# A two-layer diffusion backbone on one core: row steps of the modulation placed behind the weight splits of the convolution, and some weight splits given to VectorE

## The chip, the cores and the metric

One core of a Trainium2 chip runs the whole kernel. The metric is the device time of one execution in microseconds. Beside it there is one execution taken by the hardware profiler, whose trace gives the start, the duration and the idle time ahead of each instruction.

## The reference

A block of two layers over 1024 latent tokens and 256 context tokens, each 1024 wide, in float32. Both streams are scaled and shifted by a modulation computed from a conditioning vector. Cut to what matters here:

```python
for layer in range(2):
    mod = silu(c) @ mod_w[layer] + mod_b[layer]            # six rows of 1024: shifts, scales, gates
    h = modulate(rms_norm(xs, norm1_g[layer]), sh1, sc1)   # hc for the context, with modc
    if layer == 0:   # gate_b, gate_c, u, q_lat, kv_lat, k_rope = split(h @ w_in)
        y = concat(gate_b * conv3(gate_c * u), latent_attention(q_lat, kv_lat, k_rope)) @ w_out
    else:
        y = window_attention(h @ w_qkv) @ w_out
    xs = xs + g1 * y
    h2 = modulate(rms_norm(xs, norm2_g[layer]), sh2, sc2)
    aff = softmax(h2 @ router_w[layer])                    # 16 experts, each takes its best 128 tokens
    g, idx = top_k(aff.T, 128)
    hid = silu(h2[idx] @ w_gate) * (h2[idx] @ w_up)        # 1024 -> 1024 for each expert
    xs = xs + g2 * scatter_add(idx, (hid @ w_down) * g)
return rms_norm(xs, final_g)                               # in layer 0 the context goes the same way
```

## The kernel before

Every float32 operand of a product is split in two: a high half (`wh`, `hh`, `xh`), which ScalarE makes by a cast, and a low half (`wl`, `hl`, `xl`), which is the operand less the high half, a subtraction on VectorE (`dve.tensor_sub`) or on GpSimd (`pool.tensor_sub`). A product is then three matmuls (`mm3`, L167 to L170): low weight by high activation, high by high, high by low. `hilo` (L163 to L165) is the pair of instructions for one tile.

The stages follow each other: the mixer of layer 0 (convolution, then latent attention), `mixer_out` of layer 0 with the routing, 16 experts, then the same in layer 1 with window attention. In the mixer of layer 0, in both `mixer_out` and in the last stage (`finish`, L2415) all queues run in the order in which the program is written. In the experts of layer 0 only TensorE and GpSimd do, and a planner lays out the other engines by its costs; in the experts of layer 1 the planner lays out everything up to `finish`. Behind the loop over the experts (L1904 and on) it lays out layer 0's queues as well.

*Start and convolution (`layer0_conv`, L415 to L655).* The tokens stand in five groups of 256 columns (`Group`); `Group.parts` (L473) scales a transposed group out of PSUM: ScalarE writes the high half (L480), VectorE writes the full value h (L484), VectorE or GpSimd subtracts (L486). The input weights come in four chunks of 384 columns and one of 416 (`Chunk`); `Chunk.parts` (L500) splits two of the eight k-blocks of a chunk, a piece. The pieces of the first chunk are split ahead of the loop, by GpSimd (L542 to L558), between the modulation's columns and the parts of the first group, and the norm of the second group (`between`, taken up a step at a time by `aside`) is started among them. The loop (L575) goes over four chunks j and over five groups g: `proj(1, g)` and `proj(2, g)` give z (L632), `proj(0, g)` gives the gate (L604), and `taps` the three-point convolution (L598 to L600). The next chunk's first two pieces are split at g = 3 (L641), the last two behind the last projection, ahead of gate(4) (L647).

Beside it the loop works off a list, `rest` (L571): eight units of TensorE for one modulation part, and four rows of modulation on VectorE. A row has four steps of four instructions (L353, `use`), each with one load in a ring of six slots, and at the end a sum over partitions by TensorE with an addition by VectorE (L361, L363, `sum`). `proj` counts its calls, and at about every second one it takes the next unit of `rest` (L590 to L593), right behind its own matmuls are queued. What is left is worked off behind the loop (L654).

*Queries (L808 to L816).* The value weights wv are split by `hilo`; the key weights wk (128 x 512) and the query weights wq (128 x 1536) are cast by ScalarE and subtracted by GpSimd, each in one piece. Beside them the last tokens' latents (L705, L720) and the norms (L177 and on) run on VectorE.

*End of mixer_out, layer 0 (L1471 to L1475).* The norms of the last two tiles, then one expert piece (128 x 2048) is split, then two more are loaded. GpSimd gathers the first expert's tokens at the same time (L1718).

*Experts.* `Weights.parts` (L1095) splits a piece of an expert's weights (L1100 ScalarE, L1101 VectorE or GpSimd); `get` hands out the next. Behind the loop, the last expert's down weights are taken in four pieces of 256 columns (wd, L1904), pieces 1 and 3 with GpSimd. `Last.choose` (L1676) makes a 0/1 matrix of the last expert's tokens (pick, on GpSimd); `down(c)` (L1912) multiplies, `put(c)` (L1922) scales a quarter and splits it (L1685, L165), `spread` and `quarter` (L1688 to L1703) bring it to its tokens by matmuls with pick. In layer 0 L1818 and L1819 are the context's silu and its product; in layer 1 `finish` orders all of it with the final norm.

## Time and profile before

| what | us |
|---|---|
| runs: lowest, median, highest | 2836.86, 2839.38, 2840.44 |
| profiled execution | 2842.59 |
| its span, first to last instruction | 2840.6 |
| TensorE busy | 2655.9 |
| VectorE busy | 2176.6 |
| ScalarE busy | 1621.3 |
| GpSimd busy | 447.5 |

The mean granted clock of TensorE over the span is 0.967 of full speed (2.4 GHz). Times of instructions are microseconds from the start of the span. In the profile PE is TensorE's matmuls, PEld its weight loads, DVE is VectorE, ACT ScalarE, POOL GpSimd, SP the engine that issues most transfers; L12 is line 12 of the kernel before.

### The profile page before, as it was taken

The numbers are of one execution on the slowest core, as the hardware profiler recorded it, in microseconds if no ns is written. First come the engines' busy times: TensorE is split into PE (matmuls) and PEld (weight loads), VectorE is DVE, ScalarE is ACT, GpSimd is POOL, SyncE is SP. The second block draws the span as 40 slices with busy tenths as digits, with TensorE's granted clock in tenths as the row PEclk, the third lists the DMA queues.
The fourth block names the chain that finished last, engine by engine and source line by source line (L and its number), as shares of the span: only waits on it lengthen the run. The fifth ranks groups of instructions, "written<-read, shape, count | busy, mean of one in ns | idle before, by whom it ended". The sixth has DMA issues, their size and how long they took to land. (4 is left out here: it accounts for less than half of the span.)

```text
span 2840.6 us, 43006 instructions
## 1 busy us (share of the span) xinstructions
PE 2655.9 (93%) x16715; PEld 2146.0 (76%) x16715; DVE 2176.6 (77%) x3423; ACT 1621.3 (57%) x2444; POOL 447.5 (16%) x298
## 2 busy tenths in 40 slices
PE   7999999999969999999999899899987799999996
PEld 5989889987757777777777677688865688877775
DVE  4775699997786676766676577799967788888887
ACT  4201577774335565655555543699933577766764
POOL 2100100000011201110201300332201522221103
PEclk8999999999989999999999999899998899999998
DMA  7552000016458878888888474311076799999993
GB/s 274 189 190 97 5 8 11 9 56 206 165 194 313 309 282 294 298 281 301 279 300 279 166 258 172 133 38 45 16 238 221 260 385 380 386 377 373 369 355 141
DMA packets 277357, 614.48 MB, mean 216 GB/s; under 512 B 25353, under 2 KB 73345, under 8 KB 275105
## 3 DMA queue, kind: packets, MB, share of 16 engines
q1 hardware_dynamic: 262000, 567.97, 55.5%
q0 software_dynamic: 15008, 43.62, 5.8%
q8 instruction: 132, 2.16, 0.3%
q14 instruction: 73, 0.59, 0.1%
q10 hardware_dynamic: 144, 0.13, 0.0%
HBM read 550.00 MB, written 61.67 MB: 215 GB/s over the span
## 5 line engine op out<-in xcount | busy, mean ns | idle before, releaser
L1101 DVE TENSOR_TENSOR wl<-raw,wh 128x2048 fp32r<-128x2048 f32 x385 | 868.6, 2283 | 265.9 <-ACT wh L1100 265.8
L1100 ACT CAST wh<-raw 128x2048 fp32r<-128x2048 f32 (+1 forms) x392 | 734.3, 1903 | 320.7 <-PE pg L1791 217.6
L1884 POOL DMA_INDIRECT acc_x<-yo,gp x30 | 108.3, 3609 | 679.3 <-DVE yo L1883 639.2
L1789 PE MATMUL pu<-wl,xh 128*128 128x512 f32 x512 | 204.5, 399 | 5.9 <-DVE wl L1101 5.9
L1787 PE MATMUL pg<-wl,xh 128*128 128x512 f32 x512 | 208.2, 407 | 0.0
L1788 PE MATMUL pg<-wh,xh 128*128 128x512 f32 x512 | 203.2, 397 | 0.0
L1792 PE MATMUL pu<-wh,xl 128*128 128x512 f32 x512 | 202.5, 395 | 0.0
L1791 PE MATMUL pg<-wh,xl 128*128 128x512 f32 x512 | 202.1, 395 | 0.0
L1790 PE MATMUL pu<-wh,xh 128*128 128x512 f32 x512 | 201.8, 394 | 0.0
L1875 PE MATMUL pd<-wl,hh 128*128 128x512 f32 x480 | 194.5, 405 | 1.2 <-ACT csl L1818 1.2
L1876 PE MATMUL pd<-wh,hh 128*128 128x512 f32 x480 | 192.1, 400 | 0.0
L1879 PE MATMUL pd<-wh,hl 128*128 128x512 f32 x480 | 150.8, 395 | 0.0
L168 PE MATMUL pc<-hT,wh 128*128 128x256 f32 x480 | 140.6, 293 | 5.5 <-ACT wh L503 3.7
L170 PE MATMUL pc<-hT,wl 128*128 128x256 f32 x480 | 138.1, 288 | 4.8 <-DVE wl L504 4.8
L169 PE MATMUL pc<-hT,wh 128*128 128x256 f32 x480 | 137.2, 286 | 0.0
L1787 PEld LDWEIGHTS pg<-wl,xh 128*128 128x128 f32 x512 | 96.7, 189 | 35.4 <-issue 12.5
L1789 PEld LDWEIGHTS pu<-wl,xh 128*128 128x128 f32 x512 | 96.7, 189 | 33.4 <-DVE wl L1101 12.1
L1796 ACT ACTIVATE sil<-pg 128x512 f32<-128x512 f32 x64 | 38.3, 599 | 139.3 <-PE pg L1791 139.3
L1812 PE MATMUL pcg<-raw,cT 128*32 128x256 f32 x2048 | 116.9, 380 | 0.1
L963 ACT CAST pt<-ppt 128x512 fp32r<-128x512 f32 (+1 forms) x192 | 95.1, 516 | 37.9 <-PE ppt L956 35.9
L967 DVE TENSOR_TENSOR pt<-ppt,pt 128x512 fp32r<-128x512 f32 (+1 forms) x192 | 110.6, 593 | 6.6 <-ACT pt L963 4.1
L1791 PEld LDWEIGHTS pg<-wh,xl 128*128 128x128 f32 x512 | 96.5, 189 | 22.9
(458 smaller groups left out, 6531.0 us busy)
## 6 DMA issues: line engine op xcount, KB each, us to landing
raw<-in_exp_w_gate_dram SPq DMA_DIRECT2D x128, 1024.0 KB
raw<-in_exp_w_up_dram SPq DMA_DIRECT2D x128, 1024.0 KB
raw<-in_exp_w_down_dram SPq DMA_DIRECT2D x128, 1024.0 KB
raw<-in_mod_w_dram SPq DMA_DIRECT2D x48, 1024.0 KB
yT<-yTd SPq DMA_DIRECT2D x17, 512.0 KB
acc_x<-xn SPq DMA_DIRECT2D x16, 512.0 KB
h2x<-h SPq DMA_DIRECT2D x16, 512.0 KB
raw<-in_w_in_dram SPq DMA_DIRECT2D x8, 768.0 KB
```

Source lines behind the costliest of these rows:

```text
L168: pe.matmul(o, ah, bl, start=first, stop=False)
L1100: act.copy(wh[:, cs], raw[:, cs])
L1101: (eng or dve).tensor_sub(wl[:, cs], raw[:, cs], wh[:, cs].bitcast(F32))
L1787: pe.matmul(pg, xh[:, k], gl[:, j], start=k == 0, stop=False)
L1788: pe.matmul(pg, xh[:, k], gh[:, j], start=False, stop=False)
L1789: pe.matmul(pu, xh[:, k], ul[:, j], start=k == 0, stop=False)
L1790: pe.matmul(pu, xh[:, k], uh[:, j], start=False, stop=False)
L1791: pe.matmul(pg, xl[:, k], gh[:, j], start=False, stop=k == 7)
L1792: pe.matmul(pu, xl[:, k], uh[:, j], start=False, stop=k == 7)
L1875: pe.matmul(pd[n], hh[k // 4][:, k % 4], w[2][:, k % 2, ns], start=k == 0, stop=False)
L1876: pe.matmul(pd[n], hh[k // 4][:, k % 4], w[1][:, k % 2, ns], start=False, stop=False)
L1879: pe.matmul(pd[n], hl[k // 4][:, k % 4], w[1][:, k % 2, ns], start=False, stop=k == 7)
```

## The change

- Start: the first chunk's four pieces are split by VectorE, and stand in another order among the first group's parts; in its first two parts ScalarE writes the first of the two h (`shared`). The squares and the norm of the second group follow behind all four parts.
- Convolution: the call that takes the next unit of `rest` becomes a function of its own (`turn`). For g = 0 of j = 1 to 3 there is one `turn` more behind gate(0), and none behind proj(0, 3) and proj(0, 4); one stands behind gate(4) and behind the two splits, of which one now comes ahead of gate(4) and one behind it. In all the loop takes 28 units instead of 29; the one that is left, the last row's sum, falls behind the loop.
- Queries: wk and wq are split by `hilo`, wq in two pieces of 768.
- End of mixer_out in layer 0: the piece is split in four quarters, and it and the two loads stand between the norms of the two tiles instead of behind both.
- Last expert of each layer: all four down pieces are split by VectorE.

```diff
--- before.py
+++ after.py
@@ -470,7 +470,7 @@
                         else:
                             pe.transpose(o, self.x[:, i, f], ident)
 
-            def parts(self, b, other=pool):
+            def parts(self, b, other=pool, shared=False):
                 todo = []
                 for i in range(2):
                     k = b * 2 + i
@@ -481,7 +481,10 @@
                     todo.append((other if i else dve, hi, lo, p, sc, sh))
                 for eng, hi, lo, p, sc, sh in todo:
                     h = cp.tile([128, 256], F32, tag="h", bufs=2, name="h")
-                    dve.tensor_scalar(h, p, sc, sh, op0=ALU.mult, op1=ALU.add)
+                    if shared and hi is todo[0][1]:
+                        act.activation(h, p, AF.Identity, scale=sc, bias=sh)
+                    else:
+                        dve.tensor_scalar(h, p, sc, sh, op0=ALU.mult, op1=ALU.add)
                     aside()
                     eng.tensor_sub(lo, h, hi.bitcast(F32))
                     aside()
@@ -539,8 +542,7 @@
         act.copy(ngc, pc[:, :8])
         first.sum()
         mb = first.mb
-        chunks[0].parts(pool)
-        chunks[0].parts(pool)
+        chunks[0].parts()
         pc = bank("B", "pcol")
         for c in range(4):
             pe.transpose(pc[:, c * 128:(c + 1) * 128], mb[:, c * 128:(c + 1) * 128], ident)
@@ -552,15 +554,16 @@
                     dve.scalar_tensor_tensor(o, view[:, s, r], 1.0, ngc.rearrange("p (j c) -> p j c", c=4), op0=ALU.add, op1=ALU.mult)
                 else:
                     dve.tensor_copy(o, view[:, s, r])
-        groups[0].parts(0, dve)
-        groups[0].parts(1, dve)
-        chunks[0].parts(pool)
-        chunks[0].parts(pool)
-        groups[1].sq(0)
+        chunks[0].parts()
+        groups[0].parts(0, dve, shared=True)
+        groups[0].parts(1, dve, shared=True)
+        chunks[0].parts()
         groups[0].parts(2)
-        groups[1].sq(1)
+        chunks[0].parts()
+        groups[0].parts(3)
+        for i in range(2):
+            groups[1].sq(i)
         between.append(groups[1].norm())
-        groups[0].parts(3)
         while between:
             aside()
         for i in range(2):
@@ -582,15 +585,19 @@
             for c in (0, NC + 1, NC + 2, NT + 3):
                 dve.memset(z[:, c:c + 1], 0.0)
 
-            def proj(f, g):
+            def turn(g=4):
+                if j or g > 1:
+                    calls[0] += 1
+                    if calls[0] % 13 % 2 == 0:
+                        next(rest, None)
+
+            def proj(f, g, aside=True):
                 p = bank("A", "pc")[:, :256]
                 for k in range(8):
                     mm3(p, w.wh[k][:, f * 128:(f + 1) * 128], w.wl[k][:, f * 128:(f + 1) * 128],
                         hT[g][0][:, k, :], hT[g][1][:, k, :], k == 0, k == 7)
-                if j or g > 1:
-                    calls[0] += 1
-                    if calls[0] % 13 % 2 == 0:
-                        next(rest, None)
+                if aside:
+                    turn(g)
                 return p
 
             def taps(zo, yo, n):
@@ -634,6 +641,8 @@
                     p = proj(0, 0)
                     taps(1, 0, NC)
                     gate(0, p)
+                    if j:
+                        turn()
                 if g == 1:
                     chunks[j + 1].load(0)
                 if g == 3:
@@ -642,11 +651,12 @@
                     chunks[j + 1].parts()
             taps(NC + 3, NC, NX)
             for g in range(1, 4):
-                gate(g, proj(0, g))
-            p = proj(0, 4)
-            chunks[j + 1].parts()
+                gate(g, proj(0, g, g < 3))
+            p = proj(0, 4, False)
             chunks[j + 1].parts()
             gate(4, p)
+            chunks[j + 1].parts()
+            turn()
             pool.dma_start(yTd[j], y)
         if "conv" in dbg:
             for j in range(4):
@@ -811,9 +821,9 @@
                 wv = [qp.tile([128, 512], F32R, name=f"wv{i}") for i in range(2)]
                 wq = [qp.tile([128, 2, 768], F32R, name=f"wq{i}") for i in range(2)]
                 hilo(wv[0], wv[1], rawk[:, 512:])
-                for w, src in ((wk, rawk[:, :512]), (wq, rawq)):
-                    act.copy(w[0], src)
-                    pool.tensor_sub(w[1], src, w[0].bitcast(F32))
+                hilo(wk[0], wk[1], rawk[:, :512])
+                for k in range(2):
+                    hilo(wq[0][:, k], wq[1][:, k], rawq[:, k])
                 tail[1].sq(1)
                 norm = tail[1].norm()
                 for i in range(2):
@@ -1101,9 +1111,9 @@
                 (eng or dve).tensor_sub(wl[:, cs], raw[:, cs], wh[:, cs].bitcast(F32))
             return raw, wh, wl
 
-        def convert(self, n, eng=None):
+        def convert(self, n, eng=None, cut=1):
             for _ in range(n):
-                self.ready.append(self.parts(self.raw.pop(0), eng))
+                self.ready.append(self.parts(self.raw.pop(0), eng, cut))
 
         def get(self, eng=None):
             if not self.ready:
@@ -1469,10 +1479,10 @@
                 next(fill, None)
             run(fill)
             if l == 0:
-                for y in tiles[8:]:
-                    y.norm()
-                W.convert(1)
+                tiles[8].norm()
+                W.convert(1, cut=4)
                 W.load(2)
+                tiles[9].norm()
                 o.scale(1)
                 for y in tiles[8:]:
                     y.mul()
@@ -1901,7 +1911,7 @@
                     xT, cT = expert(e, xT, cT)
                 e = E - 1
                 hh, hl, chT, ctx_rest = expert(e, xT, cT)
-            wd = [W.get(pool if c % 2 else None) for c in range(4)]
+            wd = [W.get() for _ in range(4)]
             last = last()
             last.choose(gi[e], mp.tile([128, NX], F32, tag="xg", bufs=XG, name="tokens"))
             W.less(mp)
```

## Rows read from the trace of the kernel before

**Rows 1.** The page, part 1: busy time of each engine, its share of the span and its number of instructions.
```profile
PE 2655.9 (93%) x16715; PEld 2146.0 (76%) x16715; DVE 2176.6 (77%) x3423; ACT 1621.3 (57%) x2444; POOL 447.5 (16%) x298
```

**Rows 2.** TensorE's waits over the whole run: what waited, for what, microseconds in total, how many times, the longest.
```profile
PE pu L1789 <- DVE wl L1101: 5.9, 9, 0.9
...
PE pc L170 <- DVE wl L504: 4.8, 2, 2.4
```

**Rows 3.** The timeline of all engines from 29 to 46 us (the start): start, duration, engine, line, operation, out<-in with shapes; in brackets the idle time ahead of it and what ended it.
```profile
30.66 3.57 POOL L504 TENSOR_TENSOR wl<-raw,wh 128x768 fp32r<-128x768 f32 x2 [29.36 <-ACT wh L503]
...
35.00 1.52 DVE L486 TENSOR_TENSOR hT<-h,hT 128x256 fp32r<-128x256 f32 x1
...
35.11 0.55 PE L168 MATMUL pc<-hT,wh 128*128 128x256 f32 x1 [3.74 <-ACT wh L503]
...
38.97 0.43 DVE L486 TENSOR_TENSOR hT<-h,hT 128x256 fp32r<-128x256 f32 x1
...
45.15 1.22 PE L469 MATMUL pxn<-dg,raw 128*128 128x128 f32 x4 [0.71 <-DVE dg L450]
```

**Rows 4.** The timeline of all engines from 300 to 322 us (the end of the latents, the values and the first queries).
```profile
306.16 3.43 POOL L816 TENSOR_TENSOR wq<-raw,wq 128x1536 fp32r<-128x1536 f32 x1 [2.46 <-PE pv L170]
...
307.93 1.69 DVE L177 TENSOR_SCALAR v<-ssl 128x4 f32<-128x4 f32 x1
...
309.64 0.44 PE L168 MATMUL pq<-wq,latT 128*128 128x384 f32 x1 [2.81 <-POOL wq L816]
...
314.65 0.34 DVE L705 SCALAR_TENSOR_TENSOR lat<-pl,y,glat 128x128 f32<-128x128 f32 x1
```

**Rows 5.** The timeline of all engines from 1563 to 1588 us (the last expert of layer 0).
```profile
1565.19 0.41 DVE L1819 TENSOR_TENSOR csl<-csl,cuc 64x256 f32<-64x256 f32 x1
...
1579.40 4.55 POOL L1101 TENSOR_TENSOR wl<-raw,wh 128x2048 fp32r<-128x2048 f32 x1 [2.81 <-ACT wh L1100]
...
1581.43 2.80 DVE L1819 TENSOR_TENSOR csl<-csl,cuc 64x256 f32<-64x256 f32 x1 [2.69 <-ACT csl L1818]
...
1584.88 0.39 PE L1920 MATMUL pd<-wh,hl 128*128 128x256 f32 x1 [1.50 <-DVE hl L165]
```

**Rows 6.** The timeline of all engines from 2786 to 2814 us (the last expert of layer 1); the last row is from the timeline of TensorE alone from 2805 us.
```profile
2795.66 2.51 DVE L1101 TENSOR_TENSOR wl<-raw,wh 128x2048 fp32r<-128x2048 f32 x1 [1.10 <-ACT wh L1100]
...
2796.07 0.39 PE L1918 MATMUL pd<-wl,hh 128*128 128x256 f32 x1 [2.16 <-POOL wl L1101]
...
2800.14 0.43 DVE L165 TENSOR_TENSOR raw<-yo,raw 128x256 fp32r<-128x256 f32 x1 [0.47 <-ACT raw L164]
...
2800.88 4.55 POOL L1101 TENSOR_TENSOR wl<-raw,wh 128x2048 fp32r<-128x2048 f32 x1
...
2801.54 4.17 DVE L165 TENSOR_TENSOR raw<-yo,raw 128x256 fp32r<-128x256 f32 x1 [0.47 <-ACT raw L164]
...
2805.86 0.77 PE L1702 MATMUL plast<-raw 128*128 128x512 f32 x1 [2.51 <-DVE raw L165]
```

**Rows 7.** Line 1101 over the whole run, by engine: durations in ns (least, median, most), start of the first and of the last, shapes.
```profile
L1101 DVE TENSOR_TENSOR wl<-raw,wh x385: 1219/2286/2699, 657.7 to 2795.7; 128x2048 fp32r<-128x2048 f32 x192, 128x1024 fp32r<-128x1024 f32 x1
...
L1101 POOL TENSOR_TENSOR wl<-raw,wh x7: 4508/4548/4637, 770.4 to 2800.9; 128x2048 fp32r<-128x2048 f32 x7
```

**Rows 8.** The windows of 27 to 51 us, of 155 to 160, of 310 to 314 and of 2806 to 2809. Columns: the stretch, its length; busy time and number of instructions of PE, PEld, DVE, ACT and POOL; the granted clock of TensorE as a share of full speed; the DMA engines' share; GB/s.
```profile
27.00:51.00 24.00, 16.64 (x64) 12.58 (x65) 15.79 (x47) 14.54 (x28) 9.54 (x7) 0.50 0.83 315
...
155.00:160.00 5.00, 3.33 (x16) 3.33 (x17) 5.00 (x11) 0.37 (x1) 0.56 (x1) 0.69 0.71 193
...
310.00:314.00 4.00, 4.00 (x16) 4.00 (x15) 3.67 (x23) 0.98 (x2) 0.00 (x0) 0.57 0.00 0
...
2806.00:2809.00 3.00, 3.00 (x11) 2.62 (x12) 1.91 (x4) 0.40 (x1) 0.00 (x0) 0.50 0.00 0
```

**Rows 9.** The timeline of all engines from 144 to 163 us (the end of the convolution's second chunk and the start of the third).
```profile
150.32 1.57 ACT L503 CAST wh<-raw 128x768 fp32r<-128x768 f32 x2 [12.93 <-PE pc L169]
...
150.49 4.87 DVE L353 SCALAR_TENSOR_TENSOR modacc<-raw,csil,modacc 128x1024 f32<-128x1024 f32 x4
...
155.66 1.82 DVE L504 TENSOR_TENSOR wl<-raw,wh 128x768 fp32r<-128x768 f32 x2
...
156.67 0.39 PE L170 MATMUL pc<-hT,wl 128*128 128x256 f32 x1 [2.43 <-DVE wl L504]
```

**Rows 10.** The timeline of VectorE from 92 to 127 us (the second chunk's first gate), and that of all engines from 115 to 127 (the first sum of a row).
```profile
119.22 0.48 DVE L604 SCALAR_TENSOR_TENSOR y<-y,cw,pc 128x256 f32<-128x256 f32 x1
...
124.21 1.06 PE L361 MATMUL pm<-modacc,ones 128*32 128x512 f32 x8
```

**Rows 11.** The timeline of all engines from 807 to 830 us (the end of layer 0's mixer_out and the start of its experts).
```profile
811.13 2.28 DVE L1101 TENSOR_TENSOR wl<-raw,wh 128x2048 fp32r<-128x2048 f32 x1
...
811.22 3.03 POOL L1718 DMA_INDIRECT xg<-h2x,gp  x1 [2.60 <-DMA gp<-lists,flat]
...
817.65 1.97 PE L410 MATMUL ptr<-ident,xg 128*128 128x128 f32 x8 [11.66 <-DMA xg<-h2x,gp]
```

**Rows 12.** Line 1718 (the gathers of xg) over the whole run, columns as in the seventh group.
```profile
L1718 POOL DMA_INDIRECT xg<-h2x,gp x32: 936/988/3030, 811.2 to 2685.1; - x32
```

**Rows 13.** The timeline of all engines from 1496 to 1503 us (the pick of tokens in layer 0).
```profile
1497.12 3.60 POOL L1679 TENSOR_SCALAR pick<-tokens,idf 128x1024 fp32r<-128x1024 f32 x1 [38.21 <-DMA tokens<-in_tokens_dram]
...
1499.23 2.28 DVE L1101 TENSOR_TENSOR wl<-raw,wh 128x2048 fp32r<-128x2048 f32 x1
```

## The prediction

> **What bounds the kernel now.** The page first: TensorE is busy for 93% of the span, so a shorter time needs either less idle time ahead of its matmuls or less of it spent at the lower of its two clocks; VectorE (77%) is next, GpSimd works for 16% [rows 1]. Then TensorE's waits over the whole run: the convolution's first projection waits 4.8 us, in two places, for VectorE's low half of a weight piece (wl), and matmuls of the experts wait nine times for a wl, 5.9 us together; that last row is what a careless change could make large [rows 2]. Then the timelines around each edited line. They show one thing in common. A VectorE instruction whose operands all lie in SBUF stands still while GpSimd runs a subtraction: the 128x256 subtraction that takes 0.43 us takes 1.52 beside GpSimd's weight pieces at the start [rows 3]; the four-element L177 begins at 307.93 and ends at 309.62, and GpSimd's wq ended at 309.59 [rows 4]; L1819 takes 2.80 instead of 0.41 and ends 0.28 us after GpSimd's wl [rows 5]; in the last expert an L165 of 0.43 takes 4.17, and ends 0.28 after GpSimd's [rows 6]. So a piece on GpSimd costs VectorE up to its own 4.5 us, and the same piece on VectorE 2.28 [rows 6, 7]. Last, the windows: a wait of TensorE of over 2 us is followed by a stretch at a lower granted clock [rows 8], so it costs more than itself.
>
> **The change part by part.** The sum is made against the profiled execution: 2842.6 us, of which 2840.6 are span. The median of the three runs lies 3.2 below it, and I take the same gain off both.
>
> *Startup.* Four weight pieces of the first chunk go from GpSimd (two in 3.57 us) to VectorE (two in 1.82 [rows 9]): VectorE gains 3.6 us of work, gives two of the first subtractions' scalings to ScalarE and loses stretches such as that of 1.1 (1.52 less 0.43) [rows 3]. Laying its queue out by hand with these durations, with wl at 30.6, 31.9, 36.3 and 39.6 between the splits of hT, the first projection (35.11 now) starts about 0.7 earlier, as the first h leaves PSUM earlier, and the norm whose scale TensorE waits for at 45.15 [rows 3] is done 1.0 to 1.45 earlier although it is now behind all the splits. TensorE runs at the 1.2 GHz clock from 27 to 51 us [rows 8], with 16.6 of 24 us busy; work pulled ahead there is done at half speed, and the clock may rise no earlier. I take **0.5** (0, if the clock's rise moves the wrong way, to 2.5: 1.45 and 1 us of low clock).
>
> *Convolution's row steps.* A row step is four L353 instructions, 4.87 us in one block on VectorE [rows 9]. In the second and third chunk one stands right ahead of the two splits: ScalarE's cast of the piece was ready at about 151.9, yet wl starts at 155.66 behind L353, which began at 150.49 [rows 9]. The change puts the splits first. The next chunk's first matmul on wl then finds the second-last piece done some 1.5 us after that chunk's start and the last one about the same, and it needs the last one 20 matmuls of 0.12 in, at 2.4. So both waits go: 4.8 [rows 2]. One is followed by the low clock: 5 us at 0.69, so 5 x 0.31 = 1.55 us lost [rows 8]. Together 6.3. What is moved: one step behind gate(4), one from proj(1,0) to proj(2,0), one to proj(0,0), and the last sum (S5) behind the whole convolution. Each step frees a slot of the ring of loads, so SP's following load moves with it by 7 us at most; by the step's distance (some 13 us a step, six slots) it still lands long ahead. Queued behind the moved blocks on VectorE are the z product and the taps; the next z has PSUM banks in hand, so TensorE doesn't wait for it. What may be late is the row sum of the second chunk: TensorE's L361 stood at 124.21, while the moved step now runs behind L604, which ends at 119.7, for 4.87, to 124.6 [rows 9, 10]: a wait of 0.4, less what the chunk itself has shifted. I subtract 0.2 (0 to 0.5). Convolution: **6.1** (4.3, if the low clock stays, to 6.4).
>
> *Query weights.* GpSimd's one wq subtraction of 3.43 us becomes two on VectorE of 0.9 each behind two casts. TensorE's wait of 2.81 ahead of the first pq goes [rows 4], and so may the 4 us at 0.57 behind it (4 x 0.43 = 1.7) [rows 8]: 4.5 at most. But VectorE gets 2.4 us of work (wk too) in a stretch where it is busy 3.67 of 4.00 [rows 8], and TensorE's next inputs come from there: the last L705 of the latents ends at 315.0 [rows 4]. It gains 1.5 from the stretched L177 and loses 2.4, so what follows is only about half as much earlier as TensorE's queue would allow: **2.3** (0.5 to 4.5).
>
> *Mixer out of layer 0.* The wl of 2.28 and GpSimd's gather of xg start together, at 811.13 and 811.22; the issue takes 3.03 [rows 11], and 0.94 to 0.99 elsewhere (32 of them, median 0.988) [rows 12]. TensorE waits 11.66 for that gather's data [rows 11]. In the new order four quarter pieces stand ahead of tile 9's norm, from 809.2 to 811.8, so the issue ends at about 812.75, 1.5 earlier, as does the landing. Then VectorE's queue, behind which the first xl stands is late next: it has the same sum of work, and gains nothing. **1.0** (-0.5, if that queue is pushed out by the norm, to 2).
> The Trainium skill ("SBUF — State Buffer", section "Who interferes with whom") says that a DVE tensor_tensor takes only the read interface that it shares with GpSimd, and that making a gather's descriptors needs the write interface, so such a subtraction does not stall the gather; it marks that as inferred. The row shows 3.03 [rows 11] beside such a subtraction, so here the measurement decides. By the rule this term would be 0 and the sum 14.6.
>
> *Last expert, layer 0.* All four down pieces go to VectorE. L1819 isn't stretched any more (2.80 to 0.41), the split of hl behind it is some 2.4 earlier, and TensorE's wait of 1.50 at 1584.88 goes [rows 5]. VectorE has to do c1 ahead of a product of sil, which it makes 0.4 late; 64 matmuls of the context lie beside it and cover that. **1.5** (0, if that cover is gone, to 3).
>
> *Last expert, layer 1.* Two waits stand on the end's path: 2.16 for GpSimd's c1 at 2796.07, and 2.51 at 2805.86 for an L165 stretched to 4.17 beside c3 [rows 6]. Behind the second the clock is 0.50 for 3 us [rows 8]: 1.5 more. The most is 6.2. VectorE takes 2 x 2.28 in exchange: c1 from about 2792, done 2 us ahead of GpSimd's, then c2 and c3 by 2800.1, in front of the puts. The last put then ends some 4 us earlier than now. **4.2** (2 to 6).
> GpSimd's pick of tokens (L1679, 3.60) may now run beside a wl; in layer 0 it did so, and the wl took its usual 2.28 [rows 13], so I add nothing.
> The same section of the Trainium skill says that a DVE instruction with two SBUF inputs contends with a GpSimd one that reads SBUF; the rows speak against it for this pair [rows 13]. By the rule a wl would end up to 3.6 later there, the sum be 12.0 and the time 2827.4, inside the forecast's range; I leave it a tenth of the forecast's chance.
>
> Sum: 0.5 + 6.1 + 2.3 + 1.0 + 1.5 + 4.2 = **15.6**. The profiled execution would take 2827.0, the median 2839.4 - 15.6 = **2823.8**. All upper ends give 2.5 + 6.4 + 4.5 + 2 + 3 + 6 = 24.4 (2815.0), all lower ends 0 + 4.3 - 0.3 + 0.5 - 0.5 + 0 + 2 = 6.0 (2833.4).
>
> **The rivals.**
> *A, slower: another order in the second layer's experts.* There a planner orders ScalarE's and VectorE's work by costs, and the costs at the end have changed (two pieces of 4.5 on GpSimd are now 2.28 on VectorE). If it lays one wl an instruction later in each of 15 experts, TensorE waits 2.28 each time: 34 us, less 15.6, so 2858. It decides from the point at which a wl has less margin than one such instruction; nine waits of 0.9 at most (5.9 in all [rows 2]) show that some have none now. Against it: the changed pieces come last, and the layer's other costs are the same.
> *B: the tails give nothing back to TensorE.* VectorE becomes the bound of both last experts: c1 and c3 ahead of the sil product and the puts, or a pick beside them. The 1.5 and 4.2 go: 9.9 are left, 2829.5. For it: in layer 1 c2 already starts only at 2795.66, so c3 lies close ahead of the puts.
> *C: only the order counts.* If VectorE's stretches beside GpSimd come back elsewhere (its other pieces stay on GpSimd, the pick and the gathers move) only the 4.8 of the convolution are left: 2834.6, no measurable change. Against it: each stretch ends with the GpSimd instruction beside it.
>
> **How the numbers follow.** A measurement of this kernel can tell about 0.2% (5.7 us) from no change. The forecast has 0.72, B 0.12, C 0.09, A 0.07. Faster: 0.84; same: 0.09; slower: 0.07. The range takes in the forecast's own ends and B, from 2815.5 to 2833.0; C and A and the last of the ends are left out.
>
> **What would show it.** TensorE's waits for wl (L504), for GpSimd's wq and wl, and for a stretched L165 gone; GpSimd's L1101 at three instead of seven and none at L504; the four L353 behind the splits; the gather's issue near 1 us; granted clock near 1 at the three stretches behind the waits. Wrong would be: new waits for a sum, for sil or hl in the last experts, or a pu wait in every expert of layer 1.

## The result, and the profile after

The changed kernel takes 2820.41 us in the median (four runs, 2819.88 to 2822.17), beside 2839.63 for the kernel before on the same chip (four runs, 2836.86 to 2840.44): a ratio of 0.9932, 95% interval 0.9920 to 0.9944, or 19.2 us less. Forecast were 15.6 us less, 2823.8, in a range of 2815.5 to 2833.0.

The profiled execution took 2820.45 us, its span 2818.7, so 21.9 less than the span before (2840.6). Page of the kernel after, part 1:

```profile
PE 2643.1 (94%) x16715; PEld 2135.2 (76%) x16715; DVE 2179.5 (77%) x3435; ACT 1622.8 (58%) x2450; POOL 417.5 (15%) x288
```

Beside [rows 1], the same 16715 matmuls are 12.8 us shorter in sum (2655.9 to 2643.1), and TensorE's time without one falls by 9.1 (184.7 to 175.6). More than half of what was won is matmuls that ran at the full clock instead of at half.

Where it was won is read from TensorE itself: for each matmul, its start in the kernel before less its start in the other kernel is the lead. The table gives the median lead of the matmuls within 6 us of a time of the kernel before, for all profiles of this study (us):

| kernel | 60 | 260 | 340 | 560 | 640 | 860 | 1560 | 1595 | 1640 | 2055 | 2100 | 2790 | 2815 |
|---|---|---|---|---|---|---|---|---|---|---|---|---|---|
| after | 2.49 | 9.42 | 11.98 | 13.55 | 13.79 | 14.36 | 14.42 | 16.13 | 16.88 | 16.97 | 17.10 | 16.94 | 21.95 |
| same_again | 0.01 | 0.02 | 0.00 | 0.03 | 0.33 | 0.10 | 0.07 | 0.08 | 0.47 | 0.17 | 0.23 | 0.20 | 0.20 |
| conv_only | 0.41 | 7.35 | 7.33 | 6.13 | 6.05 | 4.64 | 4.70 | 4.70 | 5.08 | 4.66 | 7.61 | 7.68 | 7.81 |
| start_only | 2.74 | 4.10 | 4.07 | 4.11 | 3.86 | 3.89 | 4.00 | 4.01 | 4.78 | 4.81 | 7.49 | 7.52 | 7.68 |
| start_pool | 0.96 | 7.90 | 10.46 | 12.01 | 12.12 | 12.30 | 12.15 | 14.01 | 13.17 | 12.75 | 15.53 | 15.74 | 20.74 |
| no_shared | 1.90 | 8.86 | 11.47 | 13.06 | 12.57 | 12.94 | 13.01 | 14.88 | 13.34 | 13.55 | 16.49 | 16.52 | 21.54 |
| c1_pool | 2.70 | 9.64 | 12.24 | 13.82 | 13.55 | 13.80 | 13.88 | 15.73 | 14.15 | 14.31 | 14.37 | 14.41 | 16.81 |
| c3_pool | 2.68 | 9.63 | 12.23 | 13.78 | 13.74 | 14.00 | 14.11 | 15.97 | 14.37 | 14.56 | 17.56 | 17.63 | 19.27 |
| ghost | 2.33 | 9.28 | 11.85 | 13.43 | 13.49 | 13.68 | 13.73 | 15.59 | 14.13 | 14.17 | 17.15 | 17.29 | 17.43 |
| mix_order | 2.14 | 9.07 | 11.62 | 13.21 | 12.91 | 13.17 | 12.99 | 14.85 | 13.22 | 13.35 | 13.17 | 13.18 | 18.20 |
| quarters_pool | 1.81 | 8.74 | 11.36 | 12.95 | 12.55 | 15.55 | 15.54 | 17.41 | 15.18 | 14.06 | 15.06 | 15.33 | 20.31 |
| quarters_dve | 2.30 | 9.24 | 11.79 | 13.35 | 13.38 | 16.27 | 16.37 | 18.24 | 18.55 | 17.07 | 20.02 | 20.05 | 25.02 |
| quarters_late | 2.07 | 9.02 | 11.57 | 13.14 | 12.88 | 15.84 | 15.83 | 17.69 | 17.99 | 16.34 | 16.35 | 16.30 | 21.28 |

The start ends by 60, the convolution by 260, the first queries by 340, the attention by 560, layer 0's mixer_out by about 800 (860 is in the first experts), layer 0's last expert by 1595, layer 1's experts run from some 2200 to 2790, and its end follows. A step between two columns is a gain or a loss in that stage.

The start, timeline of all engines from 27 to 52 us, and the windows of 27 to 51 and of 48 to 51; beside [rows 3, 8]:

```profile
29.51 0.69 DVE L308 TENSOR_TENSOR modb<-pm,modb 128x512 f32<-128x512 f32 x1 [17.90 <-PE pm L304]
...
30.61 0.96 DVE L507 TENSOR_TENSOR wl<-raw,wh 128x768 fp32r<-128x768 f32 x1 [0.41 <-ACT wh L506]
...
33.26 0.43 DVE L489 TENSOR_TENSOR hT<-h,hT 128x256 fp32r<-128x256 f32 x1 [0.53 <-ACT h L485]
...
34.29 0.55 PE L168 MATMUL pc<-hT,wh 128*128 128x256 f32 x1 [2.92 <-DVE h L487]
...
43.48 3.78 PE L469 MATMUL pxn<-dg,raw 128*128 128x128 f32 x16 [1.10 <-DVE dg L450]
```

```profile
27.00:51.00 24.00, 16.29 (x85) 13.20 (x86) 16.11 (x53) 15.65 (x30) 3.48 (x4) 0.64 0.83 315
...
48.00:51.00 3.00, 3.00 (x28) 3.00 (x27) 2.14 (x10) 1.37 (x3) 1.47 (x2) 1.00 0.00 0
```

In the kernel before, timeline from 28 to 46 us and window of 48 to 51:

```profile
29.51 0.69 DVE L308 TENSOR_TENSOR modb<-pm,modb 128x512 f32<-128x512 f32 x1 [17.90 <-PE pm L304]
```

```profile
48.00:51.00 3.00, 3.00 (x16) 3.00 (x15) 2.65 (x10) 2.31 (x5) 0.74 (x1) 0.50 0.01 3
```

VectorE's low half of a piece takes 0.95, its 128x256 subtraction 0.43, with no weight piece of GpSimd's beside it. L308 is the last instruction of VectorE ahead of all that is edited, and it starts at 29.51 in both kernels. The first projection starts at 34.29 instead of 35.11, and the matmuls with dg at 43.48 instead of 45.15. The window has a granted clock of 0.64 instead of 0.50, and 85 matmuls instead of 64 lie in it; from 48 to 51 the clock is full, where it was 0.50. The change brings a wait too: GpSimd's first 128x256 subtraction (38.37) starts inside VectorE's split of the last piece (38.13) and takes 1.29 instead of 0.73, and TensorE waits 1.22 for it.

The end of the convolution's second chunk, timeline from 146 to 158 us, beside [rows 9]:

```profile
147.83 1.57 ACT L506 CAST wh<-raw 128x768 fp32r<-128x768 f32 x2 [12.93 <-PE pc L169]
...
148.70 0.96 DVE L507 TENSOR_TENSOR wl<-raw,wh 128x768 fp32r<-128x768 f32 x1 [0.23 <-ACT wh L506]
...
150.11 0.48 DVE L611 SCALAR_TENSOR_TENSOR y<-y,cw,pc 128x256 f32<-128x256 f32 x1 [0.45 <-PE pc L170]
...
150.51 0.95 DVE L507 TENSOR_TENSOR wl<-raw,wh 128x768 fp32r<-128x768 f32 x1
...
151.38 4.87 DVE L353 SCALAR_TENSOR_TENSOR modacc<-raw,csil,modacc 128x1024 f32<-128x1024 f32 x4
...
151.59 0.28 PE L170 MATMUL pc<-hT,wl 128*128 128x256 f32 x1
```

Cast, split, gate, split, and only then the four L353: the next chunk's matmul on wl follows without a wait at 151.59.

The first queries, timeline from 296 to 300 us and window of 297 to 302, beside [rows 4, 8]:

```profile
296.08 1.83 DVE L165 TENSOR_TENSOR wq<-raw,wq 128x768 fp32r<-128x768 f32 x2 [2.61 <-ACT wq L164]
...
297.28 0.33 PE L168 MATMUL pq<-wq,latT 128*128 128x384 f32 x1
...
298.63 0.16 DVE L177 TENSOR_SCALAR v<-ssl 128x4 f32<-128x4 f32 x1
```

```profile
297.00:302.00 5.00, 4.16 (x22) 3.44 (x22) 4.25 (x22) 3.86 (x14) 0.00 (x0) 1.00 0.00 0
```

No wait ahead of pq, L177 takes 0.16 instead of 1.69, and the clock is full where it was 0.57.

The end of layer 0's mixer_out, timeline from 790 to 816 us, beside [rows 11, 12]:

```profile
795.47 2.49 DVE L1111 TENSOR_TENSOR wl<-raw,wh 128x512 fp32r<-128x512 f32 x4
797.52 1.28 POOL L1728 DMA_INDIRECT xg<-h2x,gp  x1 [2.59 <-DMA gp<-lists,flat]
...
802.24 1.97 PE L410 MATMUL ptr<-ident,xg 128*128 128x128 f32 x8 [9.93 <-DMA xg<-h2x,gp]
...
807.49 0.50 PE L1801 MATMUL pg<-wh,xl 128*128 128x512 f32 x1 [1.66 <-DVE xl L165]
```

The gather's issue takes 1.28 instead of 3.03 and TensorE's wait for its data is 1.7 shorter; but a wait of 1.66 for VectorE's xl has come in behind it.

Layer 0's last expert, timeline from 1562 to 1572 us, beside [rows 5]:

```profile
1567.02 0.38 PE L1928 MATMUL pd<-wl,hh 128*128 128x256 f32 x1 [1.60 <-ACT csl L1828]
...
1567.14 0.41 DVE L1829 TENSOR_TENSOR csl<-csl,cuc 64x256 f32<-64x256 f32 x1
```

L1829 (L1819 before) takes 0.41 instead of 2.80, so the wait of 1.50 for hl is gone; one of 1.60, for ScalarE's csl, stays (1.65 before).

Layer 1's last expert, timeline from 2776 to 2788 us, and window of 2785 to 2788, beside [rows 6, 8]:

```profile
2777.82 0.39 PE L1928 MATMUL pd<-wl,hh 128*128 128x256 f32 x1 [0.85 <-DVE wl L1111]
...
2778.73 2.29 DVE L1111 TENSOR_TENSOR wl<-raw,wh 128x2048 fp32r<-128x2048 f32 x1 [0.36 <-ACT wh L1110]
...
2781.33 2.28 DVE L1111 TENSOR_TENSOR wl<-raw,wh 128x2048 fp32r<-128x2048 f32 x1
...
2783.53 0.42 DVE L165 TENSOR_TENSOR raw<-yo,raw 128x256 fp32r<-128x256 f32 x1
...
2785.39 0.48 PE L1712 MATMUL plast<-raw 128*128 128x512 f32 x1 [0.30 <-DVE raw L165]
```

```profile
2785.00:2788.00 3.00, 2.70 (x19) 2.46 (x19) 2.27 (x5) 0.41 (x1) 0.00 (x0) 1.00 0.01 3
```

The wait for piece 1 is 0.85 instead of 2.16, the one at the first plast 0.30 instead of 2.51, and the clock behind it is full instead of 0.50.

### The profile page after: what moved, and what is told of

It reads as the page before. It is cut to its first block, busy times and chain, and to the rows that moved or that the text cites. A ratio compares the mean times of both kernels' runs of the same rounds, so it can differ in the third digit from the quotient of the medians.

```text
span 2818.7 us, 43003 instructions
## 1 busy us (share of the span) xinstructions
PE 2643.1 (94%) x16715; PEld 2135.2 (76%) x16715; DVE 2179.5 (77%) x3435; ACT 1622.8 (58%) x2450; POOL 417.5 (15%) x288
## 3 DMA queue, kind: packets, MB, share of 16 engines
q8 instruction: 132, 2.16, 0.3%
## 5 line engine op out<-in xcount | busy, mean ns | idle before, releaser
L1111 DVE TENSOR_TENSOR wl<-raw,wh 128x2048 fp32r<-128x2048 f32 x392 | 878.3, 2268 | 264.0 <-ACT wh L1110 264.0
```

Of the source, the lines that this page charges most:

```text
L1111: (eng or dve).tensor_sub(wl[:, cs], raw[:, cs], wh[:, cs].bitcast(F32))
```

## The experiments

**same_again**: the kernel before, unchanged.

> The kernel before, unchanged. Its first profiled execution took 2842.59 us, 3.0 above the median of its runs, and the span of the changed kernel is 21.9 us shorter than that one, while the medians lie only 19.2 apart. Theory (some 3 us of the 21.9 are the spread from one execution to the next): this profile is up to 3 us shorter than the first, in one or two places that the change does not touch, and each stage that the change touches keeps its length within 0.3. Rival (the profiled stages are exact, and the spread lies outside the span): the same span within 0.5, and no stage moves.

Span 2840.4 (2840.6 the first time), no stage moved by more than 0.5; ten runs with a median of 2840.92 beside 2842.23 of 22 runs of the kernel before that were taken with them, ratio 0.9995 (0.9985 to 1.0005). The theory falls: this profile repeats the first.

**conv_only**: the kernel before with `turn` and the moved splits alone (the end of the edit; `turn` itself and the call behind gate(0) are those of the change).

```diff
-                gate(g, proj(0, g))
-            p = proj(0, 4)
-            chunks[j + 1].parts()
+                gate(g, proj(0, g, g < 3))
+            p = proj(0, 4, False)
             chunks[j + 1].parts()
             gate(4, p)
+            chunks[j + 1].parts()
+            turn()
```

> The kernel before with the row steps' part alone. Theory (local terms that add up): the two waits of 4.8 us together and the stretch of low clock at 157 go, as in the changed kernel, where TensorE's lead grows from 2.5 us at the convolution's start to 9.5 at its end; so a lead of 6.3 to 7.0 at the convolution's end here too, kept to the end of the span, and a time of about 2833. Rival (the steps fit behind the splits only because the start gives VectorE 2.5 us of lead): one of the waits or the wait for the first row's sum stays, the lead is below 4.8, time above 2834.5.

Median 2834.20 beside 2842.23, ratio 0.9968 (0.9957 to 0.9980). Both waits for wl are gone, and the lead grows by 6.94 up to 260 (7.35 - 0.41), with no lead from the start: as the theory has it; in the changed kernel it is 6.93. The rival falls. That lead isn't kept as it was: up to 860 2.7 us are lost and at 2100 3.0 are won, in stages that this kernel doesn't touch.

**start_only**: the kernel before with the start's part alone.

> The kernel before with the start's part alone. Theory: a lead of 2.5 us at 60 us as in the changed kernel, kept through the convolution to the end, as TensorE is busy there without a break; about 2837. Rival (the convolution's splits stand at a place that VectorE sets): the lead is used up at the waits for wl at 157 or 208 us, which become longer by it, and the end moves by less than 1.

Median 2837.64, ratio 0.9984 (0.9974 to 0.9994). The lead at 60 is 2.74 and is not used up: the two waits for wl are still 4.8 in sum, and the stretch of low clock behind the first of them didn't come here, so the lead is 4.10 at 260. The rival falls.

**start_pool**: the changed kernel with the four pieces on GpSimd again.

```diff
-        chunks[0].parts()
+        chunks[0].parts(pool)
```

(at all four places.)

> The changed kernel with the first chunk's four pieces split by GpSimd again, in the new order and with ScalarE's share of the h. Theory (what counts at the start is that no GpSimd subtraction stands beside VectorE's): the 128x256 subtractions take 1.2 to 1.5 again, the waits of the first projection return, and at least 2 of the 2.5 us of lead at 60 us are lost. Rival (the order and ScalarE's share of the h bring the lead): at least 1.5 of the 2.5 stay.

One execution, 2821.82. Timeline of this kernel from 28 to 46 us:

```profile
28.77 0.69 DVE L308 TENSOR_TENSOR modb<-pm,modb 128x512 f32<-128x512 f32 x1 [17.01 <-PE pm L304]
...
30.62 3.57 POOL L507 TENSOR_TENSOR wl<-raw,wh 128x768 fp32r<-128x768 f32 x2 [29.32 <-ACT wh L506]
...
32.68 1.79 DVE L489 TENSOR_TENSOR hT<-h,hT 128x256 fp32r<-128x256 f32 x1 [2.08 <-ACT h L485]
...
36.21 1.77 DVE L489 TENSOR_TENSOR hT<-h,hT 128x256 fp32r<-128x256 f32 x1
...
45.25 1.01 PE L469 MATMUL pxn<-dg,raw 128*128 128x128 f32 x3 [1.30 <-DVE dg L450]
```

The stretched subtractions are back (1.79 and 1.77), the lead at 60 is 0.96: 1.5 of 2.5 lost, between the two expectations. But that lead also holds what was there ahead of the edits: L308 starts at 28.77 in this profile, 0.74 earlier than in the kernels before and after. From L308 to the matmuls with dg it takes 16.48 here, 13.97 in the kernel after and 15.64 in the kernel before. So with the pieces on GpSimd nothing of the start's gain is left, and of the 0.96 only 0.2 came behind L308: the theory holds and the rival falls. **no_shared**, all h of the first group on VectorE, tells what ScalarE's share of the h is worth.

```diff
-        groups[0].parts(0, dve, shared=True)
-        groups[0].parts(1, dve, shared=True)
+        groups[0].parts(0, dve)
+        groups[0].parts(1, dve)
```

> The changed kernel with all h of the first group on VectorE, as before the change. With GpSimd in place of VectorE for the pieces, 1.5 to 1.8 of the start's 2.5 us of lead went. Theory (the rest, 0.7 to 1.0, comes from ScalarE's share of the h): the first projection starts 0.5 to 1 later and the lead at 60 us is 0.5 to 1 less. Rival (it comes from the order, with the norm of the second group behind the parts): the lead at 60 us is the same within 0.3.

One execution, 2820.88. The first projection starts 0.27 later (34.56) and the lead at 60 is 1.90, but L308 is 0.15 later too (29.66). From L308 the first projection is 0.12 later (4.90 beside 4.78), less than expected, and the matmuls with dg are 0.57 later (14.54 beside 13.97; 13.97 to 14.18 in all nine profiles with the whole of the start's part). So ScalarE's share is worth 0.4 to 0.6 at dg. What it is worth at 60 isn't shown: the same nine profiles have leads from 1.81 to 2.74 there, and 1.90 lies among them. What the order alone is worth isn't shown either.

**c1_pool** and **c3_pool**: in layer 1, piece 1 or piece 3 of the last down weights on GpSimd again.

```diff
-            wd = [W.get() for _ in range(4)]
+            wd = [W.get(pool if c == 1 and l == 1 else None) for c in range(4)]
```

> The changed kernel with piece 1 of the last expert's down weights of layer 1 on GpSimd again. In the changed kernel VectorE splits it from 2775.5 to 2777.8 and TensorE waits 0.85 for it at 2777.8. Theory (TensorE waits for GpSimd's 4.55): the wait is 2.0 to 2.2 again, and the lead behind it 1.3 us less. Rival (VectorE's queue is what counts there): freed of 2.28, VectorE finishes c2 and the puts earlier, and the lead is the same or grows.

One execution, 2825.61. Timeline of this kernel from 2776 to 2788 us:

```profile
2781.66 0.58 PE L1928 MATMUL pd<-wl,hh 128*128 128x256 f32 x1 [2.15 <-POOL wl L1111]
```

TensorE waits 2.15 for the piece, 1.3 longer, and its next matmuls take 0.41 instead of 0.28. From 2790 to 2815 the lead grows by 2.40 instead of 5.01. The wait is the theory's; with the low clock behind it the cost is 2.6, twice what I had expected. The rival falls.

> The changed kernel with piece 3 of the last expert's down weights of layer 1 on GpSimd again. Nobody waits for that piece itself: TensorE needs it some 5 us later. Theory (GpSimd's subtraction holds VectorE's up): the first put's L165 of 0.42 takes about 4 us again, TensorE waits 2.5 for it and runs at the low clock behind it; 3.7 us of lead are lost. Rival (VectorE is short of time at the end, and what it saves of 2.28 counts): the lead is the same or larger.

One execution, 2823.13. Timeline of this kernel from 2778 to 2790 us:

```profile
2779.91 4.89 POOL L1111 TENSOR_TENSOR wl<-raw,wh 128x2048 fp32r<-128x2048 f32 x1 [19.68 <-ACT wh L1110]
...
2781.20 3.88 DVE L165 TENSOR_TENSOR raw<-yo,raw 128x256 fp32r<-128x256 f32 x1 [0.47 <-ACT raw L164]
...
2786.51 0.47 PE L1712 MATMUL plast<-raw 128*128 128x512 f32 x1 [2.12 <-DVE raw L165]
```

L165 takes 3.88 beside GpSimd's piece, TensorE waits 2.12, and the lead grows by 1.64 instead of 5.01: 3.4 lost (3.7 expected). The rival falls: with 2.28 less to do, VectorE is later.

**ghost**: a GpSimd subtraction that nobody reads, at the same place.

```diff
+                idle = fp.tile([128, 7, 256], F32R, name="idle")
...
                 r = {}
+                pool.tensor_sub(idle, w3[0][:, :7], w3[1][:, :7].bitcast(F32))
                 down(0, range(4))
```

(w3 is piece 3 of wd.)

> The changed kernel with one GpSimd subtraction added that nobody reads: seven eighths of piece 3 of layer 1's last down weights, raw less high, into a tile of its own, as soon as ScalarE has made the high half (about 2780.5, 4.0 us long). VectorE, ScalarE and TensorE have the same instructions in the same order as before it. Theory (the hold-up alone, with no result to wait for, costs the time): VectorE's own subtraction of piece 3, which starts at 2781.3, or the L165 behind it, is stretched by 3 us or more, and TensorE waits at the first matmuls of plast; 3 to 5 us of lead are lost. Rival (only the wait for GpSimd's late result cost anything): no wait, within 0.3 us of the changed kernel's lead.

One execution, 2825.12. Timeline of this kernel from 2780 to 2792 us:

```profile
2780.25 4.34 POOL L2468 TENSOR_TENSOR idle<-raw,wh 128x1792 fp32r<-128x1792 f32 x1 [19.68 <-ACT wh L1110]
...
2780.98 5.76 DVE L1111 TENSOR_TENSOR wl<-raw,wh 128x2048 fp32r<-128x2048 f32 x1
...
2788.51 0.77 PE L1712 MATMUL plast<-raw 128*128 128x512 f32 x1 [3.77 <-DVE raw L165]
```

GpSimd begins at 2780.25, VectorE's own wl 0.73 later, and that takes 5.76 instead of 2.28: it ends 2.15 after GpSimd's end at 2784.59, about its own length. So VectorE did nothing of it in between. TensorE waits 3.77 at plast, and the lead grows by 0.14 instead of 5.01 at the end: 4.9 lost to a result that nobody uses. The rival is refuted. The Trainium skill ("SBUF — State Buffer", section "Who interferes with whom") says that a DVE instruction with two SBUF inputs contends with a GpSimd instruction that reads SBUF; the 5.76 here agree.

**mix_order**: the piece at the end of layer 0's mixer_out in one instruction, at its new place.

```diff
-                W.convert(1, cut=4)
+                W.convert(1)
```

> The changed kernel with the piece at the end of layer 0's mixer_out split in one instruction of 2.28 instead of four, at its new place between the norms of the two tiles. Theory (the gather's issue waits for a subtraction that stands beside it, whatever its length): the piece now ends ahead of or during the issue, so the issue takes 1.0 to 2 us and the lead at 850 us differs by less than 0.5. Rival (it is the cut into four that lets the issue in): the issue takes 2 to 3 us again, and the gather lands 1 us later or more.

One execution, 2824.26. Timeline of this kernel from 795 to 805 us, and then one of the kernel before from 2286 to 2292:

```profile
796.42 2.28 DVE L1111 TENSOR_TENSOR wl<-raw,wh 128x2048 fp32r<-128x2048 f32 x1
798.47 1.08 POOL L1728 DMA_INDIRECT xg<-h2x,gp  x1 [2.59 <-DMA gp<-lists,flat]
...
802.97 1.97 PE L410 MATMUL ptr<-ident,xg 128*128 128x128 f32 x8 [9.71 <-DMA xg<-h2x,gp]
```

```profile
2288.30 2.28 DVE L1101 TENSOR_TENSOR wl<-raw,wh 128x2048 fp32r<-128x2048 f32 x1
2288.77 2.66 POOL L1718 DMA_INDIRECT xg<-h2x,gp  x1 [23.63 <-PE ptr L410]
```

The subtraction ends at 798.70, the issue that starts at 798.47 takes 1.08, and TensorE waits 9.71. From 640 to 860 the lead grows by 0.26, in the changed kernel by 0.57. The place is what counts, the cut brings nothing that one execution can show. The kernel before has the same thirteen times more, in layer 1's experts: an issue in front of which a subtraction of 2.28 was started 0.47 to 0.59 earlier takes 2.54 to 2.66 and ends 0.82 to 0.86 behind the subtraction. Seventeen of its 32 issues take 0.94 to 1.0; at one of them (828.29) a subtraction starts 0.41 behind the issue. Most of the 3.75 by which this profile ends behind the changed kernel's comes from stages that the two have in common (the columns up to 640, and 1595 to 1640).

**quarters_pool**, **quarters_dve**, **quarters_late**: GpSimd's remaining piece in layer 0's mixer_out (line 1460 after), beside which L1245 takes 4.30. In quarters on GpSimd (the edit shown); in quarters on VectorE; in quarters on GpSimd, one line later.

```diff
-                    W.convert(1, pool)
+                    W.convert(1, pool, cut=4)
                     yield from rest
```

> The changed kernel with GpSimd's remaining piece in layer 0's mixer_out (128 x 2048, ahead of the last two tiles' products) split in four quarters. There an addition of 0.69 on VectorE (xn, L1245) takes 4.30 beside it, TensorE waits 4.2 for its result and then runs 6.8 us at the low clock. Theory (VectorE is held for one GpSimd instruction, and gets its turn between two): the addition takes 1.8 at most, the wait falls to about 1.5, and with a part of the low clock 3 to 6 us are gained: about 2816. Rival (GpSimd's queue keeps its hold over four instructions): still 3.5 to 4.3, no gain.

> The changed kernel with that same piece on VectorE in four quarters of 0.6, at the same place of the order. Theory: VectorE is busy 2.4 us ahead of the product for xn instead of being held 3.6, so TensorE's wait of 4.2 falls to about 3, and the low clock behind it stays; 1 to 2 us gained, about 2819; the routing's chain on VectorE moves with it. Rival (the routing's chain of small instructions sets this stage): the chain is 2.4 longer and nothing is gained.

> The changed kernel with that piece in four quarters on GpSimd, behind the eighth tile's steps instead of ahead of them. Theory: the wait of 4.2 goes altogether, with the low clock behind it: 5 to 7 us gained, about 2814, unless another VectorE instruction with its operands in SBUF now stands beside a quarter (then at most 1.1 us of it comes back at each). Rival (ScalarE's four casts, which move too, or the load of the next piece come late): a wait for wl of the first expert, and less than 3 us gained.

Medians 2821.04, 2818.72 and 2821.31 (four runs each), ratios to the kernel before 0.9923 (0.9907 to 0.9940), 0.9920 (0.9904 to 0.9937) and 0.9928 (0.9912 to 0.9945): none can be told from the changed kernel's 0.9932. Timeline of the kernel after from 752 to 772 us, then that of quarters_late from 759 to 772 and its window of 765 to 775:

```profile
756.71 4.52 POOL L1111 TENSOR_TENSOR wl<-raw,wh 128x2048 fp32r<-128x2048 f32 x1 [158.92 <-DVE rids L1586]
757.47 4.30 DVE L1245 TENSOR_TENSOR xn<-xn,xt 128x512 f32<-128x512 f32 x1
```

```profile
759.13 0.63 PE L1279 MATMUL pxT<-ident,xn 128*128 128x128 f32 x4 [0.59 <-DVE xn L1245]
...
761.03 6.95 POOL L1111 TENSOR_TENSOR wl<-raw,wh 128x512 fp32r<-128x512 f32 x4 [162.33 <-ACT wh L1110]
...
761.33 2.08 DVE L1224 TENSOR_TENSOR yl<-yT,yh 128x1024 fp32r<-128x1024 f32 x1
...
763.34 2.30 DVE L1264 TENSOR_TENSOR h<-h,B 128x1024 f32<-128x1024 f32 x1
...
771.23 1.08 PE L1279 MATMUL pxT<-ident,xn 128*128 128x128 f32 x4 [5.89 <-DVE xn L1245]
```

```profile
765.00:775.00 10.00, 4.11 (x23) 2.83 (x25) 9.69 (x53) 1.31 (x3) 2.98 (x2) 0.68 0.73 243
```

The wait of 4.2 fell as the theory says: to 0.95, 2.99 and 0.59. Of the 2.8 us that quarters_late is ahead of the changed kernel there, 0.8 are left 11 us later: TensorE now waits 5.89 at 771.23 for the next xn, which comes 0.8 earlier than in the changed kernel, for VectorE is busy for 9.69 of 10 us with the routing's chain. Most of the wait was moved on to the engine that sets this stage. Of the 2.3 to 2.4 us by which their lead grows more from 640 to 860 than the changed kernel's, 0.6 to 0.8 are there at 800; the rest comes at 830 to 833, where the changed kernel's profile has a stretch of low clock and theirs have none. That is hardly chance of one profile: their lead grows by 2.9 to 3.0 in that stage, and in all seven profiles that have the changed mixer_out without the quarters by 0.18 to 0.57. So the quarters do gain some 2.4 us up to 860; why the stretch of low clock is missing there isn't shown, and the medians can't show the gain. My expectations counted the wait and not who comes next.

## Why the prediction was right, and where its sizes were off

| part | forecast | measured (steps of the lead) | in all profiles that have the part |
|---|---|---|---|
| start | 0.5 (0 to 2.5) | 2.5 | 1.8 to 2.7 |
| convolution | 6.1 (4.3 to 6.4) | 6.9 | 6.9 to 7.0 |
| query weights | 2.3 (0.5 to 4.5) | 2.6, and 1.6 in the attention | 2.5 to 2.6, and 1.6 |
| mixer out, layer 0 | 1.0 (-0.5 to 2) | 0.6 | 0.2 to 0.6 (2.9 to 3.0 with the quarters) |
| last expert, layer 0 | 1.5 (0 to 3) | 1.7 | 1.7 to 1.9 |
| last expert, layer 1 | 4.2 (2 to 6) | 5.0 | 5.0 |
| stages without an edit | 0 | 1.1 | -2.5 to 1.9 |
| sum | 15.6 | 21.95 of the span, 19.2 of the medians | |

Every part with an edit but the mixer_out, which is hardly clear of its spread, came out with the sign that was forecast, by the waits that were named, and was worth more than forecast. How near the sum came is in part luck, for the stages that were put at 0 come to anything between -2.5 and 1.9 from one profile to the next. In the sum of the lower ends stands a 0.3 that no part names; the forecast and the range don't hang on it.

*The start.* The mechanism was right, the term mis-sized: "work pulled ahead there is done at half speed, and the clock may rise no earlier". The clock did rise earlier: it is full from 48 to 51 us, where it was 0.50. The matmuls with dg come 1.67 earlier, beside 1.0 to 1.45 forecast. In start_only the lead is as large. Up to dg the whole gain goes with GpSimd's pieces (start_pool); without ScalarE's share 0.4 to 0.6 of it go (no_shared).

*The convolution.* Both waits went, and the one stretch of low clock: 6.9 where the sum has 6.3. The wait that I subtracted for the first row's sum (0.2) is not among TensorE's waits in the kernel after. The rest of 0.6 is no spread, for this step is 6.93 to 6.96 in all eleven profiles with the part: the first place gives 4.2 and the second 2.75, the second 0.35 more than its wait of 2.4, and that isn't traced further. The stretch of low clock was taken a little short, since it goes on behind the window's end at 160 (0.96 from 160 to 165). The prediction opens by saying that a wait of over 2 us is followed by a stretch at a lower clock; the second of these two waits was not, and no low clock stood behind it to be won. conv_only shows that this part stands alone.

*The query weights.* TensorE's queue would have allowed 4.5, and 2.6 came through; that VectorE would hold it back, as argued, is half of it. The first new wait is 0.84 at 300.63, for ScalarE's copy of pq out of PSUM (L856), which the forecast didn't count; the second is 0.35 at 308.56, for VectorE's kT (L730). What the forecast lacked besides is a second stretch of low clock in the attention behind it: the window of 340 to 350 us has a granted clock of 0.83 in the kernel before, the same work in the kernel after (328 to 338) 1.00. All ten profiles with this part gain 1.55 to 1.59 there and none of the three without it does; why the clock stays up isn't shown.

*Mixer out.* The issue is shorter as forecast, and VectorE's queue, which the prediction has as "late next", is what the 1.66 for xl are. But the term is too large, for the lead grows by 0.2 to 0.6 in that stage with the part and by -1.4, -0.2 and 0.0 in the three profiles without it, which is hardly clear of its spread. The prediction also misread [rows 12]: 0.988 is the median of the 32 issues and not their upper end, and fifteen of them take 1.8 to 3.0. Against the rule of the Trainium skill that I had weighed ("SBUF — State Buffer", section "Who interferes with whom"), the issue falls from 3.03 to 1.28 as soon as the subtraction is moved ahead of it, and to 1.08 in mix_order.

*The last experts.* The waits went. In layer 0 the 1.7 to 1.9 are often not kept: in six of the ten profiles with this part a stretch of low clock that lasts longer than before takes them back between 1595 and 1640, so that -0.4 to 0.4 are left of them at 1640, no more than the 0.4 to 0.8 by which the lead grows there without the part. In layer 1 VectorE's piece 1 still costs 0.85; ghost and c3_pool show that the hold alone was worth 3.4 to 4.9 there, c1_pool that the late result was worth 2.6. These overlap, since each of the three kernels has one stretch of low clock behind its wait and the kernel before has one in all, so they don't add up to the 5.0. As to the pick, for which the prediction added nothing: in layer 0 the wl beside it takes 2.28 again, in layer 1 one takes 3.13 (2758.18), and from 2100 to 2790 the lead moves by no more than 0.16.

*The rivals.* A: between 1640 and 2790 the lead stays at 16.9, so no expert of layer 1 was laid out worse. B: the tails gave 1.7 and 5.0. C: the steps outside the convolution come to 15.0, and ghost shows that VectorE's stretches beside GpSimd cost time of themselves.

What stays open: why the medians lie 19.2 apart and the spans 21.9. The difference lies with the kernel before: its profiled execution took 2842.59 beside a median of 2839.63, that of the kernel after 2820.45 beside 2820.41. In the later series its median was 2842.23 (22 runs) and 2842.04 (7 runs); what sets it isn't known. The same kernel's profile repeats (same_again), yet among the profiles the stage from 2055 to 2100, which no kernel here edits, is worth about 0 in some and 2.7 to 3.0 us in others (once 1.0). Single profiles with such steps can't say what share of the 1.1 in unedited stages belongs to the change.

## What to carry to other kernels

Before giving GpSimd a subtraction to relieve VectorE, look at what VectorE does beside it with operands in SBUF: in the last expert of layer 1 a piece of 4.55 us on GpSimd cost more than one of 2.28 on VectorE, whoever needed the result. Price a wait of TensorE with the stretch of low clock behind it, which here cost from nothing (the convolution's second wait) to as much as the wait again (c1_pool). And before removing a wait look for the engine that releases the next one: where VectorE was busy for 97% of a stage, 2.0 of 2.8 us won were lost 11 us later. A step of the lead at the place of an edit isn't yet time won at the end: look again behind the next stretch of low clock.

## What the runs showed of the hardware that was not expected

The window of 2062 to 2074 us of the kernel after, in layer 1's mixer_out, and then that of the same matmuls in no_shared, 2064 to 2074.6 (columns as in the eighth group of rows):

```profile
2062.00:2074.00 12.00, 9.68 (x41) 7.58 (x39) 7.15 (x22) 3.75 (x8) 0.00 (x0) 0.86 0.97 325
```

```profile
2064.00:2074.60 10.60, 8.28 (x41) 6.32 (x39) 6.62 (x22) 3.84 (x8) 0.00 (x0) 1.00 1.08 365
```

The same code runs at a granted clock of 0.86 in one profile and at 1.00 in the other, though the two kernels differ in the first 60 us alone: the same 41 matmuls take 12.0 us in the one and 10.6 in the other. That is a part of the 2.9 us between the columns 2055 and 2100, which is more than several parts of this change, and one profile can hide or feign that much.

Four GpSimd subtractions in a row give VectorE a turn between them, and both sides pay: in quarters_late VectorE's L1224 and L1264 take 2.08 and 2.30 instead of 1.21 and 1.22, and GpSimd's four 6.95 together instead of 4.52 for the one.
